# A convolution layer's first stage in a fused decoder kernel: norm and scaling in PSUM, split weights stored and read back, 16 taps on TensorE, layer norm's scale kept in PSUM

## The chip, the cores and the metric

The kernel runs on one core of a Trainium2 chip. A core has five engines with a queue each, worked in order: TensorE (PE, with its weight loads shown apart as PEld), VectorE (DVE), ScalarE (ACT), GpSimd (POOL) and SyncE (SP), which here issues every DMA. SBUF holds the tiles; PSUM has eight banks of 128 x 512 float32, which PE writes. The metric is the device time of one execution in microseconds (us).

## The reference, cut to what matters

Two layers over 1024 tokens of 1024 channels, in float32. The first layer's mixer is a convolution module, and it is the part that changes:

```python
hn = rms_norm(h, norm_mix_g[0])
u = hn @ w_pw1 + b_pw1                       # 1024 -> 2048
u = jax.nn.glu(u, axis=-1)                   # a * sigmoid(b)
u = causal_depthwise_conv(u, w_dw) + b_dw    # 31 taps in each channel
u = jax.nn.silu(layer_norm(u, ln_g, ln_b))
h = h + u @ w_pw2 + b_pw2
h = h + sqrelu_mlp(rms_norm(h, norm_ffn_g[0]), w1[0], w2[0])
```

Behind it come the second layer (a gated delta rule and an MLP) and a final norm.

## The kernel before

Everything is kept with channels on partitions: a tile is 128 channels by 512 tokens, so a half of the sequence (`hf` 0 or 1) has eight tiles. The stage runs in this order of code: pw1 of half 0, pw1 of half 1, layer norm of half 0, pw2 of half 0, then the first MLP of half 0, beside which half 1's convolution and layer norm run. A tile scheduler sets the order in each engine's queue when the kernel is built; each queue is then worked in that order.

**Products.** Each output tile is one `product` (L161): 8 blocks of 128 channels, and three matmuls for each, since every float32 operand is split in a high and a low part (L175 wh x hi, L176 wh x lo, L177 wl x hi): 24 matmuls of 128 x 512. In half `hf`, pw1 has `pa{hf}_{ct}` and `pb{hf}_{ct}` for ct 0 to 7, 16 products; their results take turns in three PSUM banks (pool `pm`). Other PSUM tiles share five banks (pool `pg`).

**Weights.** `weights` (L110) loads 512 KB of a weight matrix (`raw`), ACT makes the high part (`wh`, L135) and DVE the low part (`wl`, L136), each with two buffers. Half 1 loads and splits the same pw1 weights again.

**The norm.** Half 0's norm is `norm_later`: the products take unscaled x, and `pa` and `pb` are multiplied by 1/rms behind it (`xa` L331, `xb` L337, into SBUF). The sum of squares is not there for the first tile's products, but is for the scaling. Half 1's norm is `norm` (L255) and runs beside half 0: `y_b` (L264) in SBUF, then split into `xn_b` (ACT's high part, DVE's low part L98).

**The gate.** ACT takes the sigmoid of pb (`sg`, L340), DVE makes u = (pa + bias) x sg (L347). The last 30 columns of half 0's u are kept in `carry` (L351) and copied ahead of half 1's u (L346), both by DVE.

**The convolution.** `CONV[hf]` gives each of the eight tiles an owner. "v": DVE, one instruction per tap (`ca`, L424), summed in PSUM. "a": ACT multiplies (`cv`, L397), POOL adds (`cp`, L399). "s": shared, DVE has the first 31 - `SHARED` taps, ACT and POOL the rest. For half 0, DVE has tiles 0, 4, 5, 6, ACT and POOL have 1, 2, 3, tile 7 is shared with 23 taps on POOL.

**The layer norm** (L436). The sum of the eight tiles (`ln`) goes through one mean (`mean_lnm`), which is subtracted (L446); ACT squares, POOL adds pairs (L450), PE gathers per-token sums (`lnv`, L224, four matmuls for each squared tile); 1/sqrt, a transposition back (`rt_ln`, L237), ACT's copy to SBUF (`rstd_ln`, L238). Even tiles are scaled by DVE (L469), odd ones by POOL (L467). Two silus on ACT (L473, L474) and a subtraction on DVE (L475) give the high and low part `la`.

**pw2** (L479) adds its product to x, which half 0 kept in SBUF (`hs[0]`).

Of the kernel before, what the change touches and what calls it, by code (L numbers as in the profile page):

```python
# [26 lines left out]

CONV = ((("v", 1), ("a", 2), ("a", 2), ("a", 2), ("v", 1), ("v", 3), ("v", 1), ("s", 1)),  # L30
        (("p", 1), ("p", 1), ("v", 3), ("v", 1), ("v", 1), ("v", 3), ("v", 1), ("p", 3)))
# [20 lines left out]
def _body(ctx, tc, a, out):  # L52
# [54 lines left out]

    keep = [f"m2_11_{NQ - 1}{o}" for o in range(KC)]

    def weights(src, name, n=KC * P):  # L110
# [22 lines left out]
        for c in range(0, KC * P, n):
            s = slice(c, c + n)
            nc.scalar.activation(out=wh[:, s], in_=raw[:, s], func=AF.Copy)  # L135
            nc.vector.tensor_tensor(out=wl[:, s], in0=raw[:, s], in1=wh[:, s].bitcast(F32),  # L136
                                    op=ALU.subtract)
# [57 lines left out]

    def weights_of(name):
        while len(split_w) < ahead[0] and plan:
# [14 lines left out]
            nc.tensor.matmul(ps, mean_w, x, start=(i == 0), stop=(i == len(parts) - 1))  # L212
# [14 lines left out]
    def rstd_of_tokens(ps, name):  # L227

        rs = sp.tile([P, NCH], F32, tag="rs", name=f"rs_{name}", bufs=2)
        nc.scalar.activation(out=rs, in_=ps[:, :NCH], func=AF.Sqrt, bias=eps[:, 0:1], scale=1.0)  # L230
# [3 lines left out]
        nc.vector.tensor_copy(r3, rs.unsqueeze(2).to_broadcast([P, NCH, P]))
        pt = pg.tile([P, NCH, P], F32, tag="pg", name=f"rt_{name}")
        for t in range(NCH):
            nc.tensor.transpose(pt[:, t, :], r3[:, t, :], ident)  # L237
        nc.scalar.activation(out=r3, in_=pt, func=AF.Copy)  # L238
# [84 lines left out]
    def pw1(hf, act, cts, acc=None):  # L323
        r = None
        for ct in cts:
            pa = dense(act, f"pa{hf}_{ct}")
            if acc is not None and r is None:
                r = rstd(mean([acc], f"p1{hf}"), f"p1{hf}")
            if r is not None:
                xx = t_tile(f"xa{hf}_{ct}")  # L330
                nc.vector.tensor_tensor(out=xx, in0=pa, in1=r, op=ALU.mult)  # L331
                pa = xx
            tick()
            pb = dense(act, f"pb{hf}_{ct}")
            if r is not None:
# [1 line left out]
                nc.vector.tensor_tensor(out=xx, in0=pb, in1=r, op=ALU.mult)  # L337
# [2 lines left out]
            nc.scalar.activation(out=sg, in_=pb, func=AF.Sigmoid,  # L340
                                 bias=col["b_pw1"][:, KC + ct:KC + ct + 1])
            u = g_tile(f"u{hf}_{ct}")
            if hf == 0:
                nc.vector.memset(u[:, 0:CP], 0.0)
            else:
                nc.vector.tensor_copy(u[:, 0:CP], carry[:, ct, :])  # L346
            nc.vector.scalar_tensor_tensor(out=u[:, CP:CP + HT], in0=pa,  # L347
                                           scalar=col["b_pw1"][:, ct:ct + 1], in1=sg,
                                           op0=ALU.add, op1=ALU.mult)
            if hf == 0:  # L350
                nc.vector.tensor_copy(carry[:, ct, :], u[:, HT:HT + CP])  # L351
# [84 lines left out]
    def layer_norm(hf, act):  # L436
        c = cs[hf]
        while any(x is None for x in c):
            yield
# [4 lines left out]
        one = KC if hf else KC - 2
        for k in range(KC):
            nc.vector.tensor_tensor(out=c[k], in0=c[k], in1=mu, op=ALU.subtract)  # L446
            sq = squares(c[k], f"ln{hf}{k}")

            if k % 2 and k < one or hf and k:
                nc.gpsimd.tensor_tensor(out=sq, in0=sq, in1=sq0, op=ALU.add)  # L450
# [8 lines left out]
        yield
        if small:  # L460
            r = rstd_of_tokens(v, f"ln{hf}")
        else:
            r = rstd(v, f"ln{hf}")
        for k in range(KC):
            b, g = col["ln_b"][:, k:k + 1], col["ln_g"][:, k:k + 1]
# [7 lines left out]
            nc.scalar.activation(out=act[k][:, 0, :], in_=c[k], func=AF.Silu, bias=b, scale=g)  # L473
# [666 lines left out]
```

## Time and profile before

| what | value |
|---|---|
| three executions | 2429.36, 2430.53, 2430.91 us |
| median | 2430.53 us |
| profiled execution, its own time | 2429.72 us |
| its span, first to last instruction | 2428.0 us |
| TensorE clock granted, mean | 0.984 |
| PE busy over the span | 2325.6 us (96%) |
| DVE, ACT, POOL busy | 1647.8, 1088.2, 617.2 us |

PE's share of 96% is a mean over all stages; the stage that is changed is the first 310 us of the span. A busy PE is not a PE at its peak: one matmul of 128 x 512 has a record of 0.39 us, and a new one starts every 0.227 us.

### The profile page before, as it was taken

How to read it: one execution, taken by the hardware profiler on the slowest of the kernel's cores; microseconds unless marked ns; L12 is line 12 of the kernel's file. 1: busy time of each engine (PE TensorE's matmuls, PEld its weight loads, DVE VectorE, ACT ScalarE, POOL GpSimd, SP SyncE). 2: the span in 40 equal slices, each digit the busy share in tenths (PEclk: the TensorE clock that was granted, in tenths of full speed). 3: DMA queues.
4: the chain of work that ended last, by engine and by line, in shares of the span. 5: the costliest groups of instructions: out<-in, count | busy, mean ns of one | idle time of the engine just before them, and what ended most of it. 6: DMA issues, size and time to landing. Idle time of an engine off the chain costs nothing. (4 is left out here: it accounts for less than half of the span.)

```text
span 2428.0 us, 30172 instructions
## 1 busy us (share of the span) xinstructions
PE 2325.6 (96%) x11412; PEld 1917.6 (79%) x11412; DVE 1647.8 (68%) x2662; ACT 1088.2 (45%) x1551; POOL 617.2 (25%) x432
## 2 busy tenths in 40 slices
PE   8698799999999989999999999899999999999998
PEld 6576677888778878888888888788888887888887
DVE  8999989645768878677544589786775446533334
ACT  6765442343636554443424365544434244432342
POOL 5998299999500100100000000001000000000000
PEclk9899899999999999999999999999999999999999
DMA  5222132333344543433334445434333343433332
GB/s 173 78 83 87 44 94 80 105 96 96 113 126 131 162 139 122 130 122 96 109 121 138 127 131 174 136 120 131 122 95 101 108 140 106 133 96 96 97 104 77
DMA packets 112961, 275.38 MB, mean 113 GB/s; under 512 B 28656, under 2 KB 30896, under 8 KB 112816
## 3 DMA queue, kind: packets, MB, share of 16 engines
q1 hardware_dynamic: 112816, 273.46, 36.3%
q8 instruction: 89, 1.46, 0.3%
q14 instruction: 56, 0.46, 0.1%
HBM read 241.92 MB, written 31.49 MB: 113 GB/s over the span
## 5 line engine op out<-in xcount | busy, mean ns | idle before, releaser
L135 ACT ACTIVATE wh_m<-raw_m 128x1024 fp32r<-128x1024 f32 x256 | 271.2, 1061 | 760.6 <-PE ps_m L176 700.1
L136 DVE TENSOR_TENSOR wl_m<-raw_m,wh_m 128x1024 fp32r<-128x1024 f32 x256 | 325.2, 1271 | 227.2 <-ACT wh_m L135 220.1
L177 PE MATMUL ps_m<-hid,wl_m 128*128 128x512 f32 (+1 forms) x1088 | 413.6, 382 | 7.6 <-DVE wl_m L136 7.5
L175 PE MATMUL ps_m<-hid,wh_m 128*128 128x512 f32 (+1 forms) x1088 | 413.4, 380 | 3.5 <-ACT hid L97 1.6
L176 PE MATMUL ps_m<-hid,wh_m 128*128 128x512 f32 (+1 forms) x1088 | 411.9, 380 | 0.0
L399 POOL TENSOR_TENSOR cp<-cp,cv 128x512 f32<-128x512 f32 x202 | 310.8, 1550 | 17.7 <-ACT cv L397 11.7
L177 PEld LDWEIGHTS ps_m<-hid,wl_m 128*128 128x128 f32 x1088 | 205.3, 189 | 47.8 <-DVE wl_m L136 12.0
L175 PEld LDWEIGHTS ps_m<-hid,wh_m 128*128 128x128 f32 x1088 | 205.3, 189 | 41.5 <-ACT wh_m L135 3.2
L176 PEld LDWEIGHTS ps_m<-hid,wh_m 128*128 128x128 f32 x1088 | 205.3, 189 | 36.9 <-issue 0.2
L175 PE MATMUL ps_m<-xn_b,wh_m 128*128 128x512 f32 x512 | 201.3, 393 | 1.0 <-ACT wh_m L135 1.0
L175 PE MATMUL ps_m<-xn_a,wh_m 128*128 128x512 f32 x512 | 200.9, 392 | 1.2 <-ACT wh_m L135 1.2
L177 PE MATMUL ps_m<-xn_a,wl_m 128*128 128x512 f32 x512 | 201.3, 394 | 0.2 <-DVE wl_m L136 0.2
L176 PE MATMUL ps_m<-xn_a,wh_m 128*128 128x512 f32 x512 | 200.9, 392 | 0.0
L176 PE MATMUL ps_m<-xn_b,wh_m 128*128 128x512 f32 x512 | 200.6, 392 | 0.0
L177 PE MATMUL ps_m<-xn_b,wl_m 128*128 128x512 f32 x512 | 200.4, 392 | 0.0
L424 DVE SCALAR_TENSOR_TENSOR ca<-u,vec,ca 128x512 f32<-128x512 f32 x268 | 188.3, 744 | 0.5
L394 POOL TENSOR_SCALAR cv<-u,vec 128x512 f32<-128x512 f32 x90 | 177.3, 1977 | 0.0
L929 POOL TENSOR_TENSOR fof<-fof,rstd_f 128x256 f32<-128x256 f32 x3 | 2.6, 890 | 581.8 <-DVE rstd_f L922 581.8
L723 POOL TENSOR_TENSOR ld<-qe,ld 128x512 f32<-128x512 f32 x16 | 21.6, 1349 | 453.6 <-ACT qe L693 418.1
L98 DVE TENSOR_TENSOR hid<-mt,hid 128x512 fp32r<-128x512 f32 x128 | 91.9, 718 | 45.2 <-ACT hid L97 44.8
L315 DVE TENSOR_TENSOR hn<-hn,ps_m 128x512 f32<-128x512 f32 x56 | 38.4, 686 | 110.8 <-PE ps_m L177 110.6
L175 PEld LDWEIGHTS ps_m<-xn_b,wh_m 128*128 128x128 f32 x512 | 96.2, 188 | 21.8 <-ACT wh_m L135 1.8
(346 smaller groups left out, 4831.2 us busy)
## 6 DMA issues: line engine op xcount, KB each, us to landing
raw_m<-w SPq DMA_DIRECT2D x256, 512.0 KB, 3.6
raw_in<-w_in SPq DMA_DIRECT2D x64, 512.0 KB, 3.6
sc<-iy SPq DMA_DIRECT2D x64, 256.0 KB, 2.1
ld<-sc SPq DMA_DIRECT2D x64, 256.0 KB, 3.9
raw_p<-w_pw SPq DMA_DIRECT2D x16, 512.0 KB, 3.6
raw_go<-w_out SPq DMA_DIRECT2D x16, 512.0 KB, 3.7
raw_pa<-w_pw SPq DMA_DIRECT2D x15, 512.0 KB, 3.6
raw_pb<-w_pw SPq DMA_DIRECT2D x15, 512.0 KB, 3.5
```

The source lines that it names most:

```text
L98: nc.vector.tensor_tensor(out=dst[:, 1, :], in0=src, in1=dst[:, 0, :].bitcast(F32), op=ALU.subtract)
L135: nc.scalar.activation(out=wh[:, s], in_=raw[:, s], func=AF.Copy)
L136: nc.vector.tensor_tensor(out=wl[:, s], in0=raw[:, s], in1=wh[:, s].bitcast(F32), op=ALU.subtract)
L175: nc.tensor.matmul(o, wh[:, s], hi, start=(k == 0), stop=False)
L176: nc.tensor.matmul(o, wh[:, s], lo, start=False, stop=False)
L177: nc.tensor.matmul(o, wl[:, s], hi, start=False, stop=last)
L315: nc.vector.tensor_tensor(out=hs[hf][o], in0=hs[hf][o], in1=ps, op=ALU.add)
L394: nc.gpsimd.tensor_scalar(out=t, in0=u[:, j:j + HT], scalar1=tap(ct, j), scalar2=None, op0=ALU.mult)
L399: nc.gpsimd.tensor_tensor(out=c, in0=c, in1=t, op=ALU.add)
L424: nc.vector.scalar_tensor_tensor(out=c if j == CW - 1 else acc, in0=u[:, j:j + HT], scalar=tap(ct, j), in1=acc, op0=ALU.mult, op1=ALU.add)
L723: nc.gpsimd.tensor_tensor(out=qT[h], in0=qe, in1=qT[h], op=ALU.mult)
L929: nc.gpsimd.tensor_tensor(out=y, in0=y, in1=r, op=ALU.mult)
```

## The change

Line numbers in the changed kernel are higher; the diff shows the code.

- *Weights.* Half 0's `dense` stores both split parts of each pw1 product's weights in DRAM (`put_weights`, 32 stores of 512 KB). Half 1 loads these parts (`weights_again`, 32 loads of 512 KB) and splits nothing. Every third product of half 1 takes the buffers of `raw`.
- *Scaling and norm in PSUM.* `pa` and `pb` of half 0 are scaled in place in their banks. Half 1's norm is `norm_first`: y is in PSUM, and so is 1/rms, which replaces the mean in its bank.
- *carry.* ACT makes the two copies.
- *x.* Half 0's x is no longer kept in SBUF: pw2 reads it again from DRAM (eight loads of 256 KB).
- *Convolution of half 0.* ACT and POOL have tiles 0, 1, 4, DVE has 2, 3, 5, tile 6 is shared with 8 taps on POOL, and tile 7 is new ("t"): DVE has its first 15 taps, PE the other 16, each as three matmuls with a diagonal matrix of the tap's weights that ACT makes (`conv_pe`).
- *Layer norm of half 0.* PE takes all eight squared tiles, with no addition on POOL; DVE scales all tiles, straight from `rt_ln` in PSUM; for odd tiles ACT has one silu and POOL makes the high part.

```diff
+CONV = ((("a", 2), ("a", 2), ("v", 1), ("v", 2), ("a", 2), ("v", 1), ("s", 1), ("t", 1)),
+SHARED = 8
+DIAG = 16
+WB = 2
...
+    def put_weights(name, parts):
+        made[name] = [dp.tile([P, KC * P], F32R, tag=f"{p}_{name}", name=f"{p}_{name}")
+                      for p in ("dh", "dl")]
+        for t, d in zip(parts, made[name]):
+            nc.sync.dma_start(d.bitcast(F32), t.bitcast(F32))
+    def weights_again(name):
+        other = list(AGAIN).index(name) % 3 == 2
+        wh = wp.tile([P, KC * P], F32R, tag="raw" if other else "wh", name=f"wh_{name}", bufs=WB)
+        wl = wp.tile([P, KC * P], F32R, tag="raw" if other else "wl", name=f"wl_{name}", bufs=WB)
+        for t, d in zip((wh, wl), made[AGAIN[name]]):
+            nc.sync.dma_start(t.bitcast(F32), d.bitcast(F32))
+        return wh, wl
...
     def dense(act, name, m=P, cols=slice(0, HT)):
-        return product(*weights_of(name), act, name, m, cols)
+        w = weights_of(name)
+        if name in AGAIN.values():
+            put_weights(name, w)
+        return product(*w, act, name, m, cols)
...
-    def rstd(ms, name):
-        r = g_tile(f"rstd_{name}")[:, :HT]
+    def rstd(ms, name, stay=False):
+        r = ms if stay else g_tile(f"rstd_{name}")[:, :HT]
...
-        nc.scalar.activation(out=r3, in_=pt, func=AF.Copy)
-        return r
+        return pt.rearrange("p c t -> p (c t)")
...
+    def norm_first(get, g, name, act):
+        acc = []
+        yield from sumsq(get, name, acc, nc.gpsimd)
+        r = rstd(mean(acc, name), name, True)
+        for k in range(KC):
+            y = pg.tile([P, HT], F32, tag="pg", name=f"y_{name}{k}")
+            nc.vector.scalar_tensor_tensor(out=y, in0=get(k), scalar=g[:, k:k + 1], in1=r,
+                                           op0=ALU.mult, op1=ALU.mult)
+            act.append(act_tile(f"xn_{name}{k}"))
+            split(act[k], y)
             yield
...
-                xx = t_tile(f"xa{hf}_{ct}")
-                nc.vector.tensor_tensor(out=xx, in0=pa, in1=r, op=ALU.mult)
-                pa = xx
+                nc.vector.tensor_tensor(out=pa, in0=pa, in1=r, op=ALU.mult)
...
-                nc.vector.tensor_copy(u[:, 0:CP], carry[:, ct, :])
+                nc.scalar.activation(out=u[:, 0:CP], in_=carry[:, ct, :], func=AF.Copy)
...
+    def conv_pe(hf):
...
+            for j in range(j0, CW):
+                dg = wp.tile([P, 2, P], F32R, tag="dg", name=f"dg{hf}_{ct}_{j}", bufs=4)
+                for i in range(2):
+                    nc.scalar.activation(out=dg[:, i], in_=ident, func=AF.Copy,
+                                         scale=wt[:, i, j:j + 1])
+                s = slice(j, j + HT)
+                nc.tensor.matmul(ps, dg[:, 0], x[:, 0, s], start=j == j0, stop=False)
+                nc.tensor.matmul(ps, dg[:, 0], x[:, 1, s], start=False, stop=False)
+                nc.tensor.matmul(ps, dg[:, 1], x[:, 0, s], start=False, stop=j == CW - 1)
...
-            if k % 2 and k < one or hf and k:
+            if hf and k:
                 nc.gpsimd.tensor_tensor(out=sq, in0=sq, in1=sq0, op=ALU.add)
...
-            if k % 2:
+            if k % 2 and not small:
                 nc.gpsimd.tensor_tensor(out=c[k], in0=c[k], in1=r, op=ALU.mult)
...
+            if k % 2 and small:
+                nc.scalar.activation(out=c[k], in_=c[k], func=AF.Silu, bias=b, scale=g)
+                nc.gpsimd.tensor_copy(act[k][:, 0, :], c[k])
```

The queues show where the moved work stands. SP, in the later part of half 0; `raw_pa_6` is the raw weights of product pa 6, `xr` a tile of x for half 1's norm. Before:

```order
L127 DMA raw_pa_5_695<-w_pw 128x1024
L304 DMA xr_543<-x 128x512
L304 DMA xr_568<-x 128x512
L127 DMA raw_pb_5_748<-w_pw 128x1024
L304 DMA xr_604<-x 128x512
L304 DMA xr_635<-x 128x512
L304 DMA xr_671<-x 128x512
L127 DMA raw_pa_6_795<-w_pw 128x1024
L127 DMA raw_pb_6_850<-w_pw 128x1024
```

And now, where `dh` and `dl` are the two stored parts in DRAM:

```order
L121 DMA dh_pb_4_748<-wh_pb_4_694 128x1024
L152 DMA raw_pb_5_800<-w_pw 128x1024
L121 DMA dl_pb_4_749<-wl_pb_4_695 128x1024
L121 DMA dh_pa_5_806<-wh_pa_5_744 128x1024
L152 DMA raw_pa_6_850<-w_pw 128x1024
L121 DMA dl_pa_5_807<-wl_pa_5_745 128x1024
L121 DMA dh_pb_5_856<-wh_pb_5_802 128x1024
L152 DMA raw_pb_6_906<-w_pw 128x1024
L121 DMA dl_pb_5_857<-wl_pb_5_803 128x1024
```

Each load of raw weights has two stores of earlier products' parts ahead of it.

PE, from the end of half 1's last product (`pb_7`) on. Before:

```order
L177 MATMUL ps_pb_7_1892<-xn_b_674,wl_pb_7_1847 128x512
L212 MATMUL mean_lnm_1781<-ln_1088,mean_w 128x512
L212 MATMUL mean_lnm_1781<-cp_7_1557,mean_w 128x512
L224 MATMUL lnv_1793<-mean_w,sq_ln_1820 128x1 x4
L224 MATMUL lnv_1793<-mean_w,sq_ln_1867 128x1 x4
L224 MATMUL lnv_1793<-mean_w,sq_ln_1909 128x1 x4
L224 MATMUL lnv_1793<-mean_w,sq_ln_1931 128x1 x4
L224 MATMUL lnv_1793<-mean_w,sq_ln_1938 128x1 x4
L237 MATMUL rt_ln_1949<-ident,rstd_ln_1947 128x128 x4
```

And now the mean, inside the product ahead of it, `pa_7`:

```order
L200 MATMUL ps_pa_7_1933<-xn_b_619,wh_pa_7_1881 128x512
L240 MATMUL mean_lnm_1861<-ln_1163,mean_w 128x512
L240 MATMUL mean_lnm_1861<-ct_7_1429,mean_w 128x512
L201 MATMUL ps_pa_7_1933<-xn_b_619,wh_pa_7_1881 128x512
L202 MATMUL ps_pa_7_1933<-xn_b_619,wl_pa_7_1882 128x512
```

and the first six of the eight groups of per-token sums, inside `pb_7`:

```order
L202 MATMUL ps_pb_7_1978<-xn_b_619,wl_pb_7_1930 128x512
L253 MATMUL lnv_1873<-mean_w,sq_ln_1875 128x1 x4
L253 MATMUL lnv_1873<-mean_w,sq_ln_1902 128x1 x4
L253 MATMUL lnv_1873<-mean_w,sq_ln_1923 128x1 x4
L253 MATMUL lnv_1873<-mean_w,sq_ln_1950 128x1 x4
L253 MATMUL lnv_1873<-mean_w,sq_ln_1966 128x1 x4
L253 MATMUL lnv_1873<-mean_w,sq_ln_1995 128x1 x4
L200 MATMUL ps_pb_7_1978<-xn_b_659,wh_pb_7_1929 128x512
```

The layer norm's work on PE stands inside half 1's last two products, where it stood behind them; in the profile each matmul of `lnv` leaves two records.

DVE, ahead of half 0's last weight splits (`wl_pa0_7`, `wl_pb0_7`). Before:

```order
L424 SCALAR_TENSOR_TENSOR ca0_4_1090<-u0_4_737,vec_96,ca0_4_1090 128x512 x4
L424 SCALAR_TENSOR_TENSOR c0_0_275<-u0_0_270,vec_96,ca0_0_274 128x512
L347 SCALAR_TENSOR_TENSOR u0_5_839<-xa0_5_786,vec_96,sg0_5_837 128x512
L331 TENSOR_TENSOR xa0_6_888<-ps_pa0_6_856,rstd_p10_220 128x512
L424 SCALAR_TENSOR_TENSOR ca0_4_1090<-u0_4_737,vec_96,ca0_4_1090 128x512
L351 COPY carry_98<-u0_5_839 128x30
L417 TENSOR_SCALAR ca0_5_1648<-u0_5_839,vec_96 128x512
L136 TENSOR_TENSOR wl_pa0_7_900<-raw_pa0_7_897,wh_pa0_7_899 128x1024
```

And now:

```order
L372 TENSOR_TENSOR ps_pa0_6_916<-ps_pa0_6_916,rstd_p10_229 128x512
L100 TENSOR_TENSOR xn_b07_689<-y_b07_685,xn_b07_689 128x512
L498 SCALAR_TENSOR_TENSOR ca0_2_541<-u0_2_537,vec_96,ca0_2_541 128x512
L385 SCALAR_TENSOR_TENSOR u0_5_895<-ps_pa0_5_810,vec_96,sg0_5_893 128x512
L498 SCALAR_TENSOR_TENSOR ca0_2_541<-u0_2_537,vec_96,ca0_2_541 128x512
L161 TENSOR_TENSOR wl_pa0_7_959<-raw_pa0_7_956,wh_pa0_7_958 128x1024
```

DVE's taps (`ca`) ahead of half 0's last split are 38 before and 14 now; ahead of the layer norm's mean they are 127 and 126.

More of the change, by code (lines that the diff above doesn't have):

```diff
@@ L108, in _body @@
     keep = [f"m2_11_{NQ - 1}{o}" for o in range(KC)]
+    AGAIN = {f"p{c}1_{ct}": f"p{c}0_{ct}" for ct in range(KC) for c in "ab"}
+    made = {}
+    def put_weights(name, parts):
[10 more added lines that the diff above has]
+        return wh, wl
     def weights(src, name, n=KC * P):
+        if name in AGAIN:
+            return weights_again(name)
         if n < KC * P:
-            raw = wp.tile([P, KC * P], F32, tag="raw", name=f"raw_{name}")
+            raw = wp.tile([P, KC * P], F32, tag="raw", name=f"raw_{name}", bufs=WB)
             nc.sync.dma_start(raw[:, :n], src)
             r3 = raw[:, :n].rearrange("p (k m) -> p k m", k=KC)
-            both = wp.tile([P, KC * P], F32R, tag="wh", name=f"wh_{name}")
+            both = wp.tile([P, KC * P], F32R, tag="wh", name=f"wh_{name}", bufs=WB)
             b4 = both.rearrange("p (k i m) -> p k i m", k=KC, i=2)
@@ L122, in weights @@
             return both, None
-        raw = wp.tile([P, KC * P], F32, tag="raw", name=f"raw_{name}")
+        raw = wp.tile([P, KC * P], F32, tag="raw", name=f"raw_{name}", bufs=WB)
         n = KC * P // (2 if name in ("pa0_0", "pb0_0") else 1)
@@ L129, in weights @@
         wh = wp.tile([P, KC * P], F32R, tag="kh" if kept else "wh", name=f"wh_{name}",
-                     bufs=KC if kept else 2)
+                     bufs=KC if kept else WB)
         wl = wp.tile([P, KC * P], F32R, tag="kl" if kept else "wl", name=f"wl_{name}",
-                     bufs=KC if kept else 2)
+                     bufs=KC if kept else WB)
         for c in range(0, KC * P, n):
@@ L350, in pw1 @@
             if hf == 0:
-                nc.vector.tensor_copy(carry[:, ct, :], u[:, HT:HT + CP])
+                nc.scalar.activation(out=carry[:, ct, :], in_=u[:, HT:HT + CP], func=AF.Copy)
             us[hf][ct] = u
@@ L360, in own_taps @@
     def own_taps(hf, ct):
-        return {"v": CW, "s": CW - SHARED}.get(CONV[hf][ct][0], 0)
+        return {"v": CW, "s": CW - SHARED, "t": CW - DIAG}.get(CONV[hf][ct][0], 0)
     def tap(ct, j):
@@ L405, in conv_pool @@
                 conv_done(hf, ct, c)
+    def conv_pe(hf):
+        for ct in conv_of(hf, "t"):
+            wt = sp.tile([P, 3, CW], F32, tag="wt", name=f"wt{hf}_{ct}")
+            wr = sp.tile([P, CW], F32R, tag="wr", name=f"wr{hf}_{ct}")
+            nc.scalar.activation(out=wr, in_=col["w_dw"][:, ct * CW:(ct + 1) * CW], func=AF.Copy)
+            nc.vector.tensor_copy(wt[:, 0], wr.bitcast(F32))
+            nc.vector.tensor_tensor(out=wt[:, 1], in0=col["w_dw"][:, ct * CW:(ct + 1) * CW],
+                                    in1=wt[:, 0], op=ALU.subtract)
+            while us[hf][ct] is None:
+                yield
+            u = us[hf][ct]
+            n = CP + HT
+            x = wp.tile([P, 2, HT + 32], F32R, tag="ux", name=f"ux{hf}_{ct}", bufs=1)
+            nc.scalar.activation(out=x[:, 0, :n], in_=u[:, :n], func=AF.Copy)
+            nc.vector.tensor_tensor(out=x[:, 1, :n], in0=u[:, :n], in1=x[:, 0, :n].bitcast(F32),
+                                    op=ALU.subtract)
+            yield
+            ps = pg.tile([P, HT], F32, tag="pg", name=f"cd{hf}_{ct}")
+            j0 = own_taps(hf, ct)
+            for j in range(j0, CW):
[7 more added lines that the diff above has]
+                nc.tensor.matmul(ps, dg[:, 1], x[:, 0, s], start=False, stop=j == CW - 1)
+                if j % 2:
+                    yield
+            c = g_tile(f"ct{hf}_{ct}")[:, :HT]
+            nc.scalar.activation(out=c, in_=ps, func=AF.Identity,
+                                 bias=col["b_dw"][:, ct:ct + 1])
+            cparts[hf][ct] = c
     def conv_vec(hf):
-        for ct in conv_of(hf, "vs"):
+        for ct in conv_of(hf, "vst"):
             while us[hf][ct] is None:
@@ L443, in layer_norm @@
         v = pg.tile([P, HT], F32, tag="pg", name=f"lnv{hf}")
-        one = KC if hf else KC - 2
         for k in range(KC):
@@ L447, in layer_norm @@
             sq = squares(c[k], f"ln{hf}{k}")
-            if k % 2 and k < one or hf and k:
+            if hf and k:
                 nc.gpsimd.tensor_tensor(out=sq, in0=sq, in1=sq0, op=ALU.add)
             sq0 = sq
-            if k == KC - 1 or not hf and (k % 2 or k >= one):
-                first, last = k == (1, KC - 1)[hf], k == KC - 1
+            if k == KC - 1 or not hf:
+                first, last = k == (0, KC - 1)[hf], k == KC - 1
                 if small:
@@ L472, in layer_norm @@
             act.append(act_tile(f"la{hf}{k}"))
-            nc.scalar.activation(out=act[k][:, 0, :], in_=c[k], func=AF.Silu, bias=b, scale=g)
-            nc.scalar.activation(out=c[k], in_=c[k], func=AF.Silu, bias=b, scale=g)
+            if k % 2 and small:
+                nc.scalar.activation(out=c[k], in_=c[k], func=AF.Silu, bias=b, scale=g)
+                nc.gpsimd.tensor_copy(act[k][:, 0, :], c[k])
+            else:
+                nc.scalar.activation(out=act[k][:, 0, :], in_=c[k], func=AF.Silu, bias=b, scale=g)
+                nc.scalar.activation(out=c[k], in_=c[k], func=AF.Silu, bias=b, scale=g)
             nc.vector.tensor_tensor(out=act[k][:, 1, :], in0=c[k],
@@ L958, in later @@
         yield from g
+    xin = [None] * KC
     fetch()
     for k in range(KC):
-        hs[0][k] = h_tile(f"h0{k}")
-        nc.sync.dma_start(hs[0][k], x_src(0, k))
+        xin[k] = h_tile(f"x0{k}")
+        nc.sync.dma_start(xin[k], x_src(0, k))
     fetch()
     xa, xb, la = [], [], []
-    acc = norm_later(h_of(0), g_of("g_mix", 0), "a0", xa)
+    acc = norm_later(lambda k: xin[k], g_of("g_mix", 0), "a0", xa)
     cv = start(conv_vec(0))
     cw = start(conv_pool(0))
-    nb = start(norm(lambda k: read(x_src(1, k), f"xr{k}"), g_of("g_mix", 0), "b0", xb, nc.gpsimd))
+    cd = start(conv_pe(0))
+    nb = start(norm_first(lambda k: read(x_src(1, k), f"xr{k}"), g_of("g_mix", 0), "b0", xb))
     pw1(0, xa, range(KC), acc)
@@ L972, in _body @@
     pw1(1, xb, range(NB))
-    finish(cv, cw)
+    finish(cv, cw, cd)
     ln = start(layer_norm(0, la))
```

7 lines of the change are left out of this document (2 added, 5 removed).

## The prediction

> **What bounds the kernel now.** I read the table of stretches first, over the stage that is changed (core 0; PE, PEld, DVE, ACT and POOL busy, granted clock, DMA share, GB/s):
>
> ```profile
> core 0: us, PE busy (x) PEld busy (x) DVE busy (x) ACT busy (x) POOL busy (x), PEclk, DMA share, GB/s
> 0.00:20.00 20.00, 10.59 (x37) 8.44 (x37) 12.57 (x12) 14.33 (x25) 10.99 (x19) 1.00 0.66 234
> 20.00:60.00 40.00, 38.03 (x161) 29.70 (x160) 35.30 (x40) 25.31 (x33) 24.68 (x18) 1.00 0.47 145
> 60.00:100.00 40.00, 26.34 (x99) 19.89 (x98) 39.93 (x43) 32.25 (x49) 34.58 (x23) 0.91 0.27 86
> 100.00:150.00 50.00, 41.76 (x162) 32.80 (x163) 49.82 (x60) 28.95 (x42) 44.68 (x30) 0.90 0.24 74
> 150.00:200.00 50.00, 46.45 (x201) 36.84 (x200) 50.00 (x64) 30.33 (x42) 49.37 (x33) 1.00 0.28 85
> 200.00:250.00 50.00, 39.94 (x164) 31.80 (x165) 40.73 (x55) 20.79 (x31) 36.59 (x24) 0.86 0.24 74
> 250.00:300.00 50.00, 38.49 (x152) 29.92 (x151) 50.00 (x66) 24.64 (x34) 12.36 (x8) 0.83 0.16 46
> ```
>
> From 60 to 200 us DVE has no idle time (39.93 of 40, 49.82 and 50.00 of 50) while PE has, so DVE sets the pace of this stage. Next, PE's timeline at the stations of the stage (start, length, line, tile; in brackets the wait and its releaser):
>
> ```profile
> 22.72 1.08 PE L212 MATMUL mean_p<-sq_a,mean_w 128*128 128x512 f32 x2
> ...
> 131.52 0.39 PE L175 MATMUL ps_pa<-xn_b,wh_pa 128*128 128x512 f32 x1
> ...
> 225.61 0.39 PE L177 MATMUL ps_pb<-xn_b,wl_pb 128*128 128x512 f32 x1
> ...
> 228.33 0.39 PE L177 MATMUL ps_pb<-xn_b,wl_pb 128*128 128x512 f32 x1
> 232.83 2.04 PE L212 MATMUL mean_lnm<-ln,mean_w 128*128 128x512 f32 x2 [4.11 <-DVE ln L377]
> 234.67 1.83 PE L212 MATMUL mean_lnm<-cp,mean_w 128*128 128x512 f32 x2
> 239.96 8.69 PE L224 MATMUL lnv<-mean_w,sq_ln 128*128 128x1 f32 x40 [3.45 <-POOL sq_ln L450]
> 249.68 1.11 PE L237 MATMUL rt_ln<-ident,rstd_ln 128*128 128x128 f32 x4 [1.03 <-DVE rstd_ln L234]
> 254.13 1.22 PE L175 MATMUL ps_p<-la,wh_p 128*128 128x512 f32 x2 [3.33 <-ACT la L473]
> ...
> 310.05 0.39 PE L175 MATMUL ps_m<-xn_a,wh_m 128*128 128x512 f32 x1
> ```
>
> Half 0 of pw1 ends at 131.5, half 1 at 228.6, pw2 starts at 254.1, the MLP at 310.05. The thirteenth matmul from 225.61 starts at 228.33, so one costs 2.72/12 = 0.227 us and a product of 24 costs 5.45. Half 0 from 22.72 would need 1.1 + 14 x 5.45 = 77.4 and took 108.8; half 1 would need 87.2 and took 97. The waits say on what:
>
> ```profile
> PE ps_pa L177 <- DVE wl_pa L136: 21.4, 12, 5.3
> PE ps_pb L177 <- DVE wl_pb L136: 5.9, 4, 2.2
> ACT sg L340 <- DVE xb L337: 10.0, 6, 2.3
> ```
>
> PE waits 27.3 us for the low part of split weights, which stands behind taps in DVE's queue.
>
> **The change, part by part.** Durations (mean ns of one, then idle time and releaser):
>
> ```profile
> L136 DVE TENSOR_TENSOR wl_pa<-raw_pa,wh_pa 128x1024 fp32r<-128x1024 f32 x15 | 25.1, 1672 | 2.1 <-ACT wh_pa L135 2.1
> L136 DVE TENSOR_TENSOR wl_pb<-raw_pb,wh_pb 128x1024 fp32r<-128x1024 f32 x15 | 23.8, 1586 | 0.0
> L346 DVE COPY u<-carry 128x30 f32<-128x30 f32 x8 | 6.6, 820 | 0.0
> L351 DVE COPY carry<-u 128x30 f32<-128x30 f32 x8 | 6.0, 746 | 0.0
> L347 DVE SCALAR_TENSOR_TENSOR u<-xa,vec,sg 128x512 f32<-128x512 f32 x8 | 10.3, 1285 | 1.8 <-ACT sg L340 1.8
> L347 DVE SCALAR_TENSOR_TENSOR u<-ps_pa,vec,sg 128x512 f32<-128x512 f32 x8 | 5.9, 739 | 0.0
> L264 DVE SCALAR_TENSOR_TENSOR y_b<-xr,vec,rstd_b 128x512 f32<-128x512 f32 x8 | 10.8, 1350 | 0.0
> L98 DVE TENSOR_TENSOR xn_b<-y_b,xn_b 128x512 fp32r<-128x512 f32 x8 | 11.4, 1421 | 0.0
> L331 DVE TENSOR_TENSOR xa<-ps_pa,rstd_p 128x512 f32<-128x512 f32 x8 | 5.5, 682 | 0.0
> L424 DVE SCALAR_TENSOR_TENSOR ca<-u,vec,ca 128x512 f32<-128x512 f32 x179 | 126.1, 744 | 0.5
> L399 POOL TENSOR_TENSOR cp<-cp,cv 128x512 f32<-128x512 f32 x112 | 173.5, 1569 | 15.5 <-ACT cv L397 11.7
> ```
>
> *DVE.* 16 weight splits of half 1 go: 16 x 1.63 = 26.1. Sixteen carry copies go to ACT: 8 x 0.82 + 8 x 0.75 = 12.6. In half 0, u reads PSUM as it does in half 1: 8 x (1.285 - 0.739) = 4.4. y_b and xn_b get one operand in PSUM; I price them at 0.74 (like u) and 0.68 (like xa): 8 x 0.61 + 8 x 0.74 = 10.8. That is 53.9 us off an engine that was full for some 205. Taps stay: 127 before the mean of the layer norm, now 126, but only 14 of them ahead of half 0's last weight split, where there were 38. POOL loses 15 adds, 15 x 1.57 = 23.6. So DVE stops being the bound in half 0: 14 splits x 1.6 + 16 scalings x 0.68 + 8 u x 0.74 + norm 11.4 + 14 taps x 0.74 + two reciprocals (about 7) come to 68 of 97 us. In half 1, 112 taps at a pitch of 0.67 = 75, with sums, u and the first taps of tiles about 90, stand against 89 us of PE: level, and I add 2 us for it.
>
> *PE, half 0.* Without waits it ends at 22.7 + 77.4 = 100.1. Added: (a) eight diagonals built on ACT ahead of the second input tile, and (b) banks. (a):
>
> ```profile
> L845 ACT ACTIVATE ys<-py 128x128 f32<-128x128 f32 x64 | 16.3, 274 | 58.7 <-PE py L843 58.6
> ```
>
> 8 x 0.274 = 2.2, partly beside the first matmuls, 0 to 2.2, taken as 1. (b) A bank of pa was free after the scaling (0.68); now it is held through scaling, sigmoid and u, and that of pb to the sigmoid. What ACT waited for xb (10.0 us) becomes a wait of PE: from 0 to 16 x 2.3 = 37 at the longest wait shown; I take the 10. (c) Waits for low parts: 21.3 of the 27.3 us fell in half 0 (the rest in half 1, which now has none); by 14 taps in place of 38 I leave 7.9. (d) The DMA. Half 0 now moves 32 stores of 512 KB, 16 weight loads, 24 loads of x: 16.8 + 8.4 + 6.3 = 31.5 MB, of which the first 20 us take some 234 x 20 = 4.7. At the rates that the rows give for a full share, 234/0.66 = 355 and 145/0.47 = 308 GB/s, the other 26.8 MB need 75 to 87 us and end at 95 to 107. That is level with PE, so I add nothing to (c) for it; its upper end, 7 us, stays in the range. All these DMAs stand in SP's one queue: a load of weights stands behind the stores of the two products before it, and so behind their splits on ACT and DVE.
>
> ```profile
> raw_pa<-w_pw SPq DMA_DIRECT2D x15, 512.0 KB, 3.6
> sc<-iy SPq DMA_DIRECT2D x64, 256.0 KB, 2.1
> ```
>
> A load lands in 3.6 us and its split follows at once; two products are in flight, 10.9 us, so loads may take more than twice that before PE sees it. Half 0 ends at 100.1 + 1 + 10 + 7.9 = 119.0 (before 131.5).
>
> The Trainium skill, "DMA: Bandwidth & Descriptors", section Specifications, has about 358 GB/s as what HBM gives one core. By that figure the 26.8 MB end at 95 and not 107; the row of 0 to 20 us agrees (355), that of 20 to 60 lies under it (308), and no run here shows stores and loads mixed at such a rate.
>
> *PE, half 1.* 16 x 5.45 = 87.2; no split, two loads of 512 KB per product, 1.05 MB in 5.45 us = 192 GB/s, below the 308. The 16 taps add 48 matmuls, 10.9. The layer norm's mean now stands inside pa 7: 1.9 (half of 3.8, since PE no longer comes to it from 4 us of rest). Six of eight groups of lnv stand inside pb 7: 48 records. At 8.69/40 = 0.217 each that is 10.4, at half of it 5.2; I take 0.15, so 7.2. With the 2 us for DVE, half 1 takes 109.2 (97 before, so longer).
>
> The Trainium skill, "TensorE: Matmul & The Clock Gate", section What's actually happening, has PE at half rate after about 3.4 us of rest; the 40 records stand behind rests of 4.11 and 3.45 us and the clock of 200 to 250 us is 0.86, which agrees. By it records between matmuls run at full rate: 5.2, not 7.2.
>
> *The tail.* Before, 228.6 to 254.1 = 25.5 us: waits, mean, squares, lnv, rsqrt, transposition, scaling, silu. Now behind the last matmul of pb 7 stand 16 records (2.4), and from lnv's end 254.13 - 248.65 = 5.5, less ACT's copy:
>
> ```profile
> 250.83 0.60 ACT L238 ACTIVATE rstd_ln<-rt_ln 128x512 f32<-128x512 f32 x1 [1.88 <-PE rt_ln L237]
> ```
>
> so 2.4 + 4.9 = 7.3. pw2 starts at 119.0 + 109.2 + 7.3 = 235.5, which is 18.6 before 254.1. POOL's conversion of four tiles is not in the trace; 0.39 us to the 1.57 of an add,
>
> ```profile
> L806 POOL COPY t6s<-T 32x256 f32<-32x256 f32 x8 | 3.1, 387 | 55.9 <-DMA T<-td 55.9
> ```
>
> against four silus less on ACT: between -1 and +4 us; taken as 0, since the later tiles are not asked for at once.
>
> *Behind it.* From pw2 on the rows are the same but for eight loads of x of 256 KB (DMA share there is 0.16): 55.9 us to the MLP as before. DVE is full from 250 to 300 us with the same work. Sum: 2429.72 (the profiled execution; span 2428.0) - 18.6 = 2411.1; the median of the three times is 0.8 above that execution, so **2412**.
>
> **Rivals.** *All covered.* Banks and splits cost PE nothing; half 0 ends where DMA does, about 103, DVE keeps up (0), lnv at full rate (5.2): 103 + 105.2 + 7.3 = 215.5, gain 38.6: 2392. For it: 30 us of room on DVE in half 0; against: three banks and the sigmoid queued among taps on ACT. *Half 0 no faster.* Banks in place of splits: 131.5 again, 131.5 + 109.2 + 7.3 = 248, gain 6: 2424. For it: xb to sigmoid to u is a chain over two full queues. *Given back.* pw2 starts early, but DVE, full from 250 to 300, sets when the MLP starts; or the eight x loads and the conversions hold pw2: 2430, the change without effect. Against it: DVE's queue is 54 us shorter by then. *Slower: the stores.* If stores and loads together run well under 308 GB/s, SP's queue delays every weight load. Half 0 may end at 119.0 + 18.6 = 137.6 before all is lost, that is 26.8 MB in 117.6 us, 228 GB/s; at 200 GB/s it ends at 154, 16.4 later: 2447. Against: 256 KB stored in 2.1 us and 512 KB loaded in 3.6; for: never both at once.
>
> **How the numbers follow.** Forecast 0.42, all covered 0.16, half 0 no faster 0.17, given back 0.10, slower 0.15. What a measurement of this kernel tells from no change is about 0.2%, 4.9 us, so 2424 is at its edge: a third of it I count as same. Faster 0.42 + 0.16 + 0.12 = 0.70, same 0.10 + 0.05 = 0.15, slower 0.15. The range, 2391 to 2438, takes in all but most of the slower case and some of the best.
>
> **What would show it.** In the changed kernel's trace: first matmul of half 1 near 119, the mean of the layer norm before pb 7 with under 3 us of wait, pw2 near 235, the MLP near 291. Wrong would be: DMA share near 1 through half 0 with its end past 135; PE waiting for sg or u by 20 us and more; a long wait at the mean (DVE late); or the MLP's start not following that of pw2.

## The result, and the profile after

| kernel | median us (lowest to highest, runs) | ratio to the kernel before, 95% interval |
|---|---|---|
| before | 2429.95 (2428.33 to 2430.91, 4) | |
| changed | 2416.14 (2410.71 to 2417.92, 4) | 0.994 (0.9928 to 0.9951) |

The change saves 13.8 us by the medians. The forecast was 2412, a gain of 18.6 us. The profiled execution of the changed kernel was the fastest of its four: 2410.71 us, 19.0 less than the profiled one of before (2429.72). So its trace shows some 5 us more gain than the median does; the other three executions were not profiled.

The table of stretches of the changed kernel, the stage in question (columns as in the prediction):

```profile
0.00:20.00 20.00, 10.38 (x30) 7.65 (x31) 10.89 (x12) 16.03 (x33) 9.06 (x18) 1.00 0.89 325
20.00:60.00 40.00, 38.33 (x163) 29.69 (x162) 22.27 (x23) 22.39 (x32) 24.72 (x18) 1.00 0.83 280
60.00:100.00 40.00, 30.44 (x109) 22.89 (x108) 26.86 (x35) 38.01 (x61) 38.46 (x28) 0.87 0.80 252
100.00:150.00 50.00, 47.57 (x200) 38.16 (x199) 46.95 (x65) 30.24 (x59) 47.65 (x35) 0.97 0.58 206
150.00:200.00 50.00, 50.00 (x222) 41.26 (x221) 50.00 (x77) 20.41 (x39) 36.57 (x29) 1.00 0.45 165
200.00:250.00 50.00, 42.04 (x188) 34.71 (x187) 31.97 (x50) 19.28 (x30) 4.27 (x4) 0.78 0.38 130
```

DVE is no longer full in half 0 (22.27 and 26.86 of 40 us); from 60 to 100 us PE still idles, but now ACT (38.01) and POOL (38.46) are nearly full, and the DMA share has gone from 0.27 to 0.80. PE's stations in the changed kernel's timeline:

```profile
24.69 1.13 PE L240 MATMUL mean_p<-sq_a,mean_w 128*128 128x512 f32 x2
...
63.84 1.41 PE L240 MATMUL mean_b<-sq_b,mean_w 128*128 128x512 f32 x2 [2.86 <-POOL sq_b L280]
...
74.90 0.79 PE L200 MATMUL ps_pb<-xn_a,wh_pb 128*128 128x512 f32 x1 [2.61 <-ACT sg L378]
...
91.64 0.62 PE L200 MATMUL ps_pb<-xn_a,wh_pb 128*128 128x512 f32 x1 [4.03 <-ACT sg L378]
92.06 0.63 PE L201 MATMUL ps_pb<-xn_a,wh_pb 128*128 128x512 f32 x1
...
124.55 0.47 PE L200 MATMUL ps_pa<-xn_b,wh_pa 128*128 128x512 f32 x1
...
216.50 1.02 PE L240 MATMUL mean_lnm<-ln,mean_w 128*128 128x512 f32 x2
...
224.16 6.37 PE L253 MATMUL lnv<-mean_w,sq_ln 128*128 128x1 f32 x48
230.40 0.77 PE L200 MATMUL ps_pb<-xn_b,wh_pb 128*128 128x512 f32 x1
...
232.68 0.63 PE L202 MATMUL ps_pb<-xn_b,wl_pb 128*128 128x512 f32 x1
233.10 3.41 PE L253 MATMUL lnv<-mean_w,sq_ln 128*128 128x1 f32 x16
...
241.03 1.22 PE L200 MATMUL ps_p<-la,wh_p 128*128 128x512 f32 x2 [2.38 <-ACT la L550]
...
293.34 0.39 PE L200 MATMUL ps_m<-xn_a,wh_m 128*128 128x512 f32 x1
```

Half 0 ends at 124.6 (before 131.5, forecast 119.0), half 1 takes 108.6 and ends at 233.1 (forecast 109.2), pw2 starts at 241.0 (forecast 235.5), the MLP at 293.3 (forecast 291). Behind the MLP's start the profiled executions need 2119.7 us before and 2117.4 now. That remainder is the same code in all kernels below and lies between 2117.4 and 2121.9 in their profiled executions: 2 us up or down say nothing.

### The profile page after: what moved, and what is told of

It reads as the page before. It is cut to its first block, busy times and chain, and to the rows that moved or that the text cites. A ratio compares the mean times of both kernels' runs of the same rounds, so it can differ in the third digit from the quotient of the medians.

```text
span 2409.0 us, 30448 instructions
## 1 busy us (share of the span) xinstructions
PE 2335.2 (97%) x11484; PEld 1930.9 (80%) x11484; DVE 1594.6 (66%) x2637; ACT 1069.9 (44%) x1566; POOL 574.3 (24%) x414
## 5 line engine op out<-in xcount | busy, mean ns | idle before, releaser
L437 POOL TENSOR_TENSOR cp<-cp,cv 128x512 f32<-128x512 f32 x187 | 275.4, 1480 | 10.9 <-ACT cv L435 3.7
L200 PEld LDWEIGHTS ps_m<-xn_a,wh_m 128*128 128x128 f32 x512 | 96.2, 188 | 21.6 <-ACT wh_m L160 2.1
```

Of the source, the lines that this page charges most:

```text
L200: nc.tensor.matmul(o, wh[:, s], hi, start=(k == 0), stop=False)
L437: nc.gpsimd.tensor_tensor(out=c, in0=c, in1=t, op=ALU.add)
```

## The experiments

Each run is told against the changed kernel unless said otherwise. Stations from each run's trace: end of half 0, start of pw2, start of the MLP.

| run | median us (runs) | ratio to before, 95% | half 0 | pw2 | MLP |
|---|---|---|---|---|---|
| before | 2429.95 | | 131.5 | 254.1 | 310.1 |
| changed | 2416.14 (4) | 0.9928 to 0.9951 | 124.6 | 241.0 | 293.3 |
| e1 no stored weights | 2424.50 (10) | 0.9968 to 0.9987 | 114.0 | 252.1 | 304.1 |
| e2 low parts only | 2409.82 (4) | 0.9901 to 0.9930 | 118.6 | 233.8 | 286.3 |
| e3 old sharing of taps | 2408.75 (4) | 0.9896 to 0.9926 | 117.6 | 237.2 | 289.2 |
| e4 old scaling and norm | 2430.02 (10) | 0.9995 to 1.0014 | 137.7 | 256.9 | 309.4 |
| e5 high parts stored by ACT | 2412.06 (4) | 0.9914 to 0.9943 | 121.4 | 241.0 | 293.5 |
| e6 old layer norm | 2413.21 (4) | 0.9916 to 0.9946 | 126.7 | 238.7 | 294.8 |
| e7 e2 and e3 | 2398.52 (4) | 0.9852 to 0.9885 | 117.8 | 227.4 | 279.0 |
| e8 e7, 15 taps on POOL | 2396.59 (4) | 0.9850 to 0.9879 | 118.6 | 222.2 | 274.1 |
| e9 stores from one tile | 2427.59 (10) | 0.9982 to 1.0001 | 139.9 | 255.1 | 307.4 |
| e10 scaled to SBUF | 2413.04 (4) | 0.9913 to 0.9942 | 121.9 | 238.4 | 290.3 |
| e11 e8, old layer norm | 2394.27 (4) | 0.9839 to 0.9872 | 118.2 | 220.0 | 274.7 |
| e12 x tiles first | 2408.81 (4) | 0.9896 to 0.9929 | 120.7 | 236.1 | 288.1 |

The changed kernel's interval overlaps those of e5, e6 and e10, and by a hair those of e2 and e12; their stations are read beside the medians.

**e1: no stored weights.**

```diff
-    AGAIN = {f"p{c}1_{ct}": f"p{c}0_{ct}" for ct in range(KC) for c in "ab"}
+    AGAIN = {}
```

> The changed kernel without the stored weights: half 1 loads and splits pw1's weights again, nothing is stored; all else as in the changed kernel. Theory A (the reuse pays by what it takes off DVE in half 1): 16 splits of 1.6 us come back on an engine whose half 1 was already level with PE, so half 1 grows by 15 to 20 us and the time is 2430 to 2436. Theory B (the reuse is nearly paid for in half 0, where 16.8 MB of stores stand in SP's queue ahead of the weight loads): half 0 ends 8 to 12 us sooner, at 113 to 117 instead of 124.6, so that only 5 to 10 us are lost: 2421 to 2426. The place of half 0's end in the trace tells them apart.

Half 0 ends at 114.0 and half 1 takes 117.4 (to 231.4): theory B. The stored weights save about 9 us in half 1 and take 10.5 in half 0. That they gain all the same, 8.4 us by the medians, comes with the layer norm, which without them stands behind half 1 and not in it: from the end of half 1 to pw2 it is 20.7 us here and 7.9 in the changed kernel.

**e2: only the low parts.**

```diff
-        for t, d in zip(parts, made[name]):
-            nc.sync.dma_start(d.bitcast(F32), t.bitcast(F32))
+        nc.sync.dma_start(made[name][1].bitcast(F32), parts[1].bitcast(F32))
...
+        raw = wp.tile([P, KC * P], F32, tag="raw", name=f"raw_{name}", bufs=WB)
+        nc.sync.dma_start(raw, src)
+        nc.scalar.activation(out=wh, in_=raw, func=AF.Copy)
```

> Only the low parts are stored and read back (16 stores of 512 KB in place of 32); half 1 loads the raw weights and ACT makes the high part again, DVE still splits nothing. Theory A (stores cost nothing): within 3 us of the changed kernel, 2413 to 2419, half 0 ends at 124 as before. Theory B (stores hold half 0): half 0 ends 4 to 8 us sooner and the time is 2408 to 2412; the spread of the single times, 7 us for the changed kernel and 2.6 for the kernel before, shrinks too if it is the DMA's.

Theory B: half 0 ends 5.9 us sooner with half the stores (10.5 with none), 2409.8. The spread did not shrink (2406.8 to 2412.9).

**e3: the old sharing of taps.**

```diff
-CONV = ((("a", 2), ("a", 2), ("v", 1), ("v", 2), ("a", 2), ("v", 1), ("s", 1), ("t", 1)),
+CONV = ((("v", 1), ("a", 2), ("a", 2), ("a", 2), ("v", 1), ("v", 3), ("v", 1), ("s", 1)),
-SHARED = 8
+SHARED = 23
```

> The convolution of half 0 is shared out as in the kernel before (DVE has tiles 0, 4, 5, 6, POOL and ACT 1, 2, 3, tile 7 is shared with 23 taps on POOL, none on TensorE); all else as changed. Theory A (TensorE's 16 taps and fewer early taps on DVE are worth their 10.9 us): PE waits for low parts in half 0 as it did before (some 10 us more), POOL's 116 adds of 1.57 us end late, the mean waits: 2420 to 2428. Theory B (the 48 matmuls of the taps cost more than they save, since DVE has lost 54 us of other work anyway): half 1 is 5 to 10 us shorter and the time is 2406 to 2412.

The time, 2408.8, is theory B's: by the medians the new sharing loses 7.4 us. PE's timeline in this run:

```profile
202.68 1.02 PE L240 MATMUL mean_lnm<-ln,mean_w 128*128 128x512 f32 x2
213.95 2.08 PE L240 MATMUL mean_lnm<-cp,mean_w 128*128 128x512 f32 x2 [7.03 <-DVE cp L507]
217.53 13.81 PE L253 MATMUL lnv<-mean_w,sq_ln 128*128 128x1 f32 x64 [1.50 <-ACT sq_ln L271]
```

As theory A said, the mean waits (7.03, for the shared tile), and 64 records behind that rest take 13.8 us. Even so pw2 starts 3.8 us sooner, and all of that comes from half 0, which ends 7 us sooner. Half 1's products, without the 48 matmuls of the taps and without the layer norm among them, end at 206.8, not at 233.1; but from the end of half 0 to pw2 it is 119.6 us here and 116.5 in the changed kernel. So the cost that theory B named, the 48 matmuls, is not what this run shows. Of the 7 us, 2.2 come ahead of the first mean (22.46 in place of 24.69), where no diagonals are built; the rest are shorter waits of PE and what follows them.

**e4: old scaling and old norm** (both in SBUF).

```diff
-                nc.vector.tensor_tensor(out=pa, in0=pa, in1=r, op=ALU.mult)
+                xx = t_tile(f"xa{hf}_{ct}")
+                nc.vector.tensor_tensor(out=xx, in0=pa, in1=r, op=ALU.mult)
+                pa = xx
...
-    nb = start(norm_first(lambda k: read(x_src(1, k), f"xr{k}"), g_of("g_mix", 0), "b0", xb))
+    nb = start(norm(lambda k: read(x_src(1, k), f"xr{k}"), g_of("g_mix", 0), "b0", xb, nc.gpsimd))
```

> Scaled pa and pb go to SBUF again and half 1's norm is the one of before (y and 1/rms in SBUF); weights, convolution, carry and layer norm as changed. Theory A (banks held longer cost PE 6.6 us of waits for the sigmoid plus cold matmuls behind them, while DVE has room in half 0): half 0 ends 3 to 8 us sooner, 2408 to 2413. Theory B (DVE's stretch by POOL comes back, about 15 us, and lands on the sigmoid and the low parts): half 0 ends 3 to 8 us later, 2419 to 2424.

Beyond theory B: 2430.0, half 0 ends 13 us later. DVE's groups from 60 to 130 us, first of the changed kernel, then of this run:

```profile
L291 DVE SCALAR_TENSOR_TENSOR y_b<-xr,vec,mean_b 128x512 f32<-128x512 f32 x8 | 5.6, 746 | 0.0
L100 DVE TENSOR_TENSOR xn_b<-y_b,xn_b 128x512 fp32r<-128x512 f32 x8 | 5.3, 671 | 0.0
L385 DVE SCALAR_TENSOR_TENSOR u<-ps_pa,vec,sg 128x512 f32<-128x512 f32 x5 | 3.7, 741 | 0.0
```

```profile
L100 DVE TENSOR_TENSOR xn_b<-y_b,xn_b 128x512 fp32r<-128x512 f32 x8 | 10.5, 1318 | 0.0
L389 DVE SCALAR_TENSOR_TENSOR u<-xa,vec,sg 128x512 f32<-128x512 f32 x5 | 7.5, 1509 | 0.0
L306 DVE SCALAR_TENSOR_TENSOR y_b<-xr,vec,rstd_b 128x512 f32<-128x512 f32 x8 | 7.4, 923 | 2.3 <-DMA xr<-x 2.3
```

The three operations cost 14.6 us with an operand in PSUM (as they were priced) and 25.4 with both in SBUF. PE's longest wait is 12.2 us for a high part on ACT, whose queue had stood 4.5 us for y_b just before and then had xn_b's high parts and taps (cv) ahead of that part.

**e10: the scaling alone to SBUF** (the first half of e4's edit).

> The changed kernel, but the scaled pa and pb of half 0 go to SBUF as before, so that their banks come free after the scaling; half 1's norm stays in PSUM. Scaling and norm together in SBUF cost 14 us. Theory A (held banks cost PE the 6.6 us of waits for the sigmoid and the cold matmuls behind them; the norm was what cost in SBUF): half 0 ends at 116 to 121, time 2408 to 2413. Theory B (u with two operands in SBUF is stretched beside POOL, 0.55 us on each of eight, and the three shared SBUF tiles for xa, xb and the sigmoid hold the chain): half 0 ends at 127 to 132, time 2419 to 2424.

Between the theories' times, near A: half 0 ends 2.7 us sooner, at 121.9, 2413.0. So what e4 lost is the norm's, and holding the banks costs some 3 us, less than the interval can tell.

**e5: high parts stored by ACT's queue.**

```diff
-        for t, d in zip(parts, made[name]):
-            nc.sync.dma_start(d.bitcast(F32), t.bitcast(F32))
+        for t, d, q in zip(parts, made[name], (nc.scalar, nc.sync)):
+            q.dma_start(d.bitcast(F32), t.bitcast(F32))
```

> As the changed kernel, but the 16 stores of high parts are issued from ACT's queue, right behind ACT's own work on them, and no longer from SP's; the same bytes move. Storing costs half 0 about 10 us (without stores it ended at 114.0, with them at 124.6). Theory A (bandwidth: DMA share 0.8 in half 0): half 0 still ends at 122 to 126, time 2413 to 2419. Theory B (SP's order: a weight load stands behind stores that wait for ACT and DVE): half 0 ends at 116 to 120, time 2407 to 2412.

Half 0 ends at 121.4, 3.2 us sooner, the median is at B's edge and the station in neither range: a share of the 10.5, not more, and the interval overlaps the changed kernel's. Inconclusive.

**e9: the same stores from one resident tile.**

```diff
-            nc.sync.dma_start(d.bitcast(F32), t.bitcast(F32))
+            nc.sync.dma_start(d.bitcast(F32), xa[0].rearrange("p i t -> p (i t)").bitcast(F32))
```

> The changed kernel with the same 32 stores of 512 KB, but their source is one resident tile (the first tile of half 0's activations) in place of the two weight parts, so that no store waits for a split or holds a weight buffer; half 1 therefore multiplies by that tile, not by the weights. Without stores half 0 ended at 114.0, with them at 124.6. Theory A (the bytes themselves: DMA's bandwidth, later x tiles): half 0 still ends at 121 to 126, time 2412 to 2418. Theory B (the order in SP's queue and the held buffers): half 0 ends at 114 to 118, time 2404 to 2409.

It missed both: as nothing held the stores, they all went ahead of the next weight loads, and PE stood 24.3 us waiting for weights. Its question stays open, but it shows what the DMA can do with stores (20 to 60 us of this run):

```profile
20.00:60.00 40.00, 16.75 (x70) 12.50 (x68) 11.45 (x9) 7.27 (x8) 4.24 (x3) 0.76 1.00 405
```

405 GB/s at full share, against 280 and 252 in the changed kernel's half 0. This is nearly all stores: 21 of the 26 transfers issued in the stretch, with the first weight load at 48.5 us. From 20 to 54 us it ran at 419 GB/s, from 54 to 60 us, with the loads, at 328 and a share of 0.88. What a full share of mixed traffic moves, the run does not show.

**e12: x tiles first.** The waits of the first 125 us gave the idea. Of the changed kernel (waiter, releaser; total, times, longest):

```profile
POOL sq_b L280 <- ACT sq_b L271: 15.2, 4, 8.1
ACT sq_b L271 <- DMA xr<-x: 12.0, 6, 4.2
PE ps_pb L200 <- ACT sg L378: 6.6, 2, 4.0
PE mean_b L240 <- POOL sq_b L280: 2.9, 1, 2.9
PE ps_pa L202 <- DVE wl_pa L161: 2.1, 2, 2.0
PE ps_pb L202 <- DVE wl_pb L161: 1.4, 2, 1.1
```

and of e1, without stores:

```profile
POOL sq_b L280 <- ACT sq_b L271: 6.5, 3, 4.1
ACT sq_b L271 <- DMA xr<-x: 3.6, 2, 2.2
PE ps_pb L200 <- ACT sg L378: 2.5, 2, 2.3
```

ACT stands in its queue at x tiles for half 1's squares, and behind them wait sigmoids, weight splits and POOL's adds. So all eight tiles were loaded ahead:

```diff
+    first = [read(x_src(1, k), f"xr{k}") for k in range(KC)]
-    nb = start(norm_first(lambda k: read(x_src(1, k), f"xr{k}"), g_of("g_mix", 0), "b0", xb))
+    nb = start(norm_first(lambda k: first.pop(0) if first else read(x_src(1, k), f"xr{k}"),
+                          g_of("g_mix", 0), "b0", xb))
```

> The changed kernel, but the eight tiles of x that half 1's squares are made of are all loaded ahead of half 0's second pair of weight stores, in one go, and no longer one by one between stores; the same bytes move. ACT waited 12.0 us for these tiles in the changed kernel, 7.4 with half the stores, 3.6 with none, and half 0 ended at 124.6, 118.6 and 114.0. Theory A (the stores' cost runs through these x tiles: squares, sigmoids and POOL's queue wait behind them): ACT waits under 4 us for x, PE does not wait for the mean, half 0 ends at 114 to 119 and the time is 2405 to 2411. Theory B (it is the weights that come late, or the bytes): half 0 still ends at 121 to 127, time 2413 to 2419.

The median, 2408.8, is A's; half 0 ends at 120.7, 1.7 us past A's range. Waits in the first 125 us of this run:

```profile
POOL sq_b L280 <- ACT sq_b L271: 4.5, 1, 4.5
PE ps_pb L200 <- ACT wh_pb L160: 4.3, 1, 4.3
PE ps_pb L200 <- ACT sg L378: 2.7, 1, 2.7
ACT wh_pa L160 <- DMA xr<-x: 0.9, 1, 0.9
```

ACT waits 0.9 us for x in place of 12.0, and PE's wait for the mean is gone. Half 0 ends 3.9 us sooner. That these 3.9 us are a part of the 10.5 that the stores cost is likely, but not shown: without stores ACT waits for x too (3.6 us in e1), and loading x first without stores was not run. Nor does this wait alone set the end of half 0. In the first 125 us ACT waits 12.6 us for x in e3 and 15.6 in e10, no less than in the changed kernel, and their half 0 ends at 117.6 and 121.9. PE has a new wait of 4.3 us for a high part; whether the x tiles now delay a weight load was not tried.

**e6: the old layer norm** (the hunks on `rstd_of_tokens` and `layer_norm` undone).

> The layer norm of half 0 as before (POOL adds pairs of squares, 20 lnv matmuls in place of 32, ACT copies the scale to SBUF, POOL scales the odd tiles, two silus on ACT for each tile); all else as changed. Theory A (the new layer norm saves a copy and POOL's slow scaling ahead of pw2): 2418 to 2422. Theory B (12 more thin matmuls at 0.13 to 0.21 us for each of two records, and the clock that falls with them, cost as much as is saved): 2412 to 2417.

2413.2, B's range, but the interval overlaps the changed kernel's, and in the traces the MLP starts 1.4 us later than there: pw2 starts 2.3 us sooner and takes 56.0 us in place of 52.3. No difference is shown.

**e7 and e8: e2 and e3 together, then 15 taps on POOL in place of 23** (`SHARED = 15`).

> Two parts together: the convolution shared out as before, and only low parts stored. Alone they gave 2408.8 and 2409.8 against 2416.1. Theory A (with the old sharing the stage ends with POOL's adds, which begin with the first tiles of half 0 and do not end sooner when half 0's products do): 2406 to 2409, half 0 ends near 113 but the mean of the layer norm still waits for DVE and POOL at 210 or later. Theory B (the two savings add): 2401 to 2404.

> As the run before, but tile 7 of half 0 is shared with 15 taps on POOL and 16 on DVE in place of 23 and 8. Theory A (POOL's adds end the stage): 8 adds of 1.57 us less on POOL, 8 taps of 0.67 more on DVE, the convolution ends 5 to 12 us sooner and the time is 2396 to 2402. Theory B (DVE's queue ends it, or POOL's end was not what counted): no change against the run before, or slower.

e7: the savings add and more, 2398.5, below both ranges; half 0 ends no sooner than in e3 (117.8), but the mean waits for nothing, and pw2 starts 9.8 us sooner than in e3. POOL began its adds 9 us sooner, since its squares came sooner: its first add is at 46.5 us here and at 55.5 in e3. e8: pw2 starts 5.2 us sooner again, and 2396.6 lies in theory A's range, but the intervals of the two runs overlap: no difference is shown. As the mean waits for nothing in e7, POOL's adds were no longer what held it.

**e11: e8 with the old layer norm.**

> The best run so far (old sharing with 15 taps of tile 7 on POOL, only low parts stored, 2396.6) with the layer norm of before. In the changed kernel the old layer norm was 2.9 us faster. Theory A (fewer thin matmuls: 40 records and not 64, and a PE clock that stays up): 2392 to 2395. Theory B (with POOL's adds ending sooner here nothing is left to gain, or POOL's scaling of the odd tiles delays pw2): 2396 to 2400.

2394.3 against 2396.6, with overlapping intervals, and the MLP starts at 274.7 against 274.1: as with e6, nothing is shown. e8 and e11 are the best versions: 33 and 36 us faster than the kernel before, 20 and 22 than the changed one.

## Why the prediction was right, and which terms were off

*DVE off the bound in half 0.* Right. From 20 to 100 us DVE is busy 22.27 and 26.86 of 40 us, where it had 35.30 and 39.93. PE's waits for low parts in half 0 are 3.6 us. 7.9 were left for them, by a share of 21.3; of these 21.3, the trace of before has 19.8 for low parts and 1.5 for a `u`. u, y_b and xn_b measure 0.741, 0.746 and 0.671 us, priced at 0.74, 0.74 and 0.68. Of the parts that were taken back, this one earns most: the norm in PSUM is worth about 17 us (2430.0 in e4 against 2413.0 in e10).

*Half 0's sum: 119.0 forecast, 124.6 measured.* The term that was mis-sized is (d), the DMA, to which nothing was added. The stores cost 10.5 us (e1) where 0 was forecast, with 7 kept for the range. The step failed because it compared bytes with a rate. The mean rate was not the limit: half 0 ran at a share of 0.83 and 0.80. What the stores lengthen is the way of single loads. Landing times up to 125 us, of the changed kernel and of e1:

```profile
raw_pa<-w_pw SPq DMA_DIRECT2D x7, 512.0 KB, 5.9
raw_pb<-w_pw SPq DMA_DIRECT2D x7, 512.0 KB, 5.1
```

```profile
raw_pa<-w_pw SPq DMA_DIRECT2D x9, 512.0 KB, 3.8
raw_pb<-w_pw SPq DMA_DIRECT2D x9, 512.0 KB, 3.6
```

The terms (a) to (c), 18.9 us, were too large for a half without stores, which takes 13.9 over its 100.1 (e1). In the changed kernel (a) is 2.0 where 1 was taken: the mean stands at 24.69 against 22.72, and e3, without diagonals, has it at 22.46. For (b) PE waits 6.6 us where 10 were taken, for (c) 3.6 where 7.9 were. Two losses had no term: the wait of 2.9 us for half 1's mean, and the matmuls behind the longer waits, which start every 0.43 us in place of 0.227 for a while (91.64 and 92.06 in the timeline above; the granted clock from 60 to 100 us is 0.87). These cost some 9.0 us, and some 9.8 in the kernel before. Together the five make 24.1 of the 24.5 us over 100.1.

PE's waits in half 0 are 13.1 us here and 6.1 in e1; the 7.0 between them are 4.1 for sigmoids and 2.9 for the mean, both behind ACT's queue, and hardly any for weights. The two sigmoids that PE waits for in the changed kernel start 7.5 and 6.1 us after DVE has scaled their banks (at 66.7 and 84.8 us), while ACT works through taps and high parts almost without a pause. The slow matmuls behind the waits cost some 3.6 us more here than in e1. So in these two traces the stores' 10.5 us reach PE through ACT, where the prediction had looked at weights alone. How the stores hold up ACT is shown in part: e12 gains 3.9 us by the order of the x tiles, e5 perhaps 3 by SP's order; the rest is not settled.

*Half 1: 109.2 forecast, 108.6 measured.* Right, and mostly by its terms. DVE was level with PE, and the mean did not wait. The 48 records inside the last product take 6.2 us (7.2 forecast, 0.13 for each), but the six matmuls behind them take 2.7 us, most of them 0.43 apart and not 0.227, which is 1.3 us more. By the rule of the Trainium skill, "TensorE: Matmul & The Clock Gate", section What's actually happening, half rate comes after about 3.4 us of rest. The trace does not agree, if rest is time without work: PE had none between 223.9 and 230.4 us, and from 230.4 to 233.1 its granted clock was 0.50.

*The tail, 7.3 forecast, 7.9 measured; pw2, 55.9 forecast, 52.3 measured.* The tail is right, pw2 was forecast 3.6 us too long. Runs with the new layer norm need 51.6 to 52.6 us for pw2, those with the old one 54.7 and 56.0; that PE waits 4.55 us there for DVE's `la`, and in the kernel before 6.3, is part of it.

*Nothing given back.* Right: the profiled gain at pw2 is 13.1 us, at the MLP 16.7, at the end 19.0.

*The taps on TensorE* were put down as 10.9 us on PE that pay by what DVE and POOL save. Against e3 they do pay behind half 0, by 3 us up to pw2, but the sharing that they belong to costs 7 us in half 0, for which the sum had only the 1 us of (a). With half the stores they do not pay behind half 0 either: from its end to pw2, e2 needs 115.2 us and e7, with the old sharing, 109.6. *The slower rival* named the right place, the stores in half 0, with the wrong means (a low rate).

*The total* is right in part by luck. In the profiled execution pw2 starts 5.5 us later than forecast, pw2 takes 3.6 us less, and the code behind it 2.3 us less, which says nothing; so 19.0 us of gain stand against 18.6. The gain by the medians, 13.8, is 4.8 less than forecast: the profiled execution ran 5 us faster than the median, for which no trace tells the reason.
